# Split mixing weights kept in HBM: the high and low parts are made once and loaded in later blocks

## Chip, core and metric

One core of a Trainium2 chip runs the whole program in one launch. The metric is the device time of one execution in microseconds; lower is better.

## The reference

One decoder layer on x of 2048 positions by 1024 channels, all in float32. Its first half, the token mixer, is where the change lies:

```python
h = rms_norm(x, norm_mix_pre)
p = h @ w_in                                  # 1024 -> 2576: u, v, q, k, b_v, g, lr
out_a = gelu(u) * spatial_gate(layer_norm(gelu(v)))    # within chunks of 128 positions
o_b = gated_linear_attention(q, k, b_v, log_sigmoid(lr @ w_gk + b_gk) / 16)
out_b = rms_norm(o_b) * silu(g)
mix = concat(out_a, out_b) @ w_out            # 1024 -> 1024
x = x + rms_norm(mix)
# then: up projection, causal convolution over 3 positions, gelu gate, down projection
x = x + rms_norm(conv_ffn(rms_norm(x)))
```

## The kernel before

**Blocks.** The mixer (`mix_phase`) works on four blocks of 512 positions, b0 to b3. In each block the normalised input lies transposed in SBUF as eight tiles of 128 channels, and every weight matrix of `w_in` and `w_out` is read from HBM again. A matrix comes in pieces of about 128 x 1024 values. A block needs 28 pieces: `g0` (2), `qk` (4), `g1` (2), `g` (4), `va` (4), `u` (4), and the two halves `mx0` and `mx1` of the output projection (8), which belong to the block before and run inside this one. The output projection of b3 has no next block: its first piece is used at the end of the mixer, the other seven at the start of the FFN phase (the tail, here), from a pool of their own.

**Split.** Matmuls run in a float32 form that keeps fewer bits, so each operand is cut in a high and a low part and a product takes three matmuls: high x high, high x low, low x high. `weight()` (L82) does this for a piece: a DMA from the queue of SP (L86) brings it into a raw tile (two buffers), ACT casts it into the high part (L89), and the low part is raw minus high (L77), made by POOL for every other piece of up to 1024 columns and by DVE for the rest. High and low tiles have three buffers each in the mixer, two each in the tail.

**Names.** In the profile a piece of the weight `gw` in block b2 is `rb2gw` (raw), `hb2gw` (high) and `lb2gw` (low). `b2g0a`, `b2g1a`, `b3mx0a` and the like are accumulators. `z`, `cum`, `kd`, `qk`, `kps`, `dps`, `lv`, `os` and `ot` are steps of the linear attention: gates (L286 to L296), decays and products with them (L440 to L468), transposes and scores on PE (L495 to L532), the normalised output (L558) and its transpose (L568). `sz` (L381) is the spatial gate, fed by the normalised `va` (L368). `h0x` to `h7x` and `h0t` to `h7t` are loads and transposes of finished positions that b3 makes for the FFN; `x0m`, `x0x` and so on are the steps of the residual sum in b1 and b2. `tal` are the loads of FFN operands in the tail.

**Order.** In the mixer a scheduler of the language sets each engine's order from estimated times; the weight steps have high priority. Each engine then works strictly in its order, and so does the queue of SP: a DMA that waits for its buffer holds all that stand behind it. The attention steps (`main`) and the weight steps (`side`) are woven by ratio, so that PE has weight matmuls to do while the others prepare attention operands. The FFN phase after the tail has a written order and is not touched.

Of the kernel before, what the change touches and what calls it, by code (L numbers as in the profile page):

```python
# [7 lines left out]
F32 = mybir.dt.float32  # L8
F32R = mybir.dt.float32r
# [8 lines left out]
P = 128  # L18
D = 1024
# [18 lines left out]
def layer_kernel(ctx, tc, x, xT, w_ch, w_gl, w_tk, w_o, w_up, w_dn, w_gk, wsT, cols, conv, rows, sgub,  # L38
                 lvl, tri, sel, out):
    nc = tc.nc  # L40
# [12 lines left out]
    def scratch(shape, name):  # L53
        return dram.tile(shape, F32, tag=name, name=name)
# [21 lines left out]
    def split_lo(eng, lo, full, hi):  # L76
        eng.tensor_tensor(out=lo, in0=full, in1=hi.bitcast(F32), op=ALU.subtract)  # L77
# [1 line left out]
    wcount = [0]  # L79
    wpool = []  # L80

    def weight(src, n, name):  # L82
        pool = wpool[-1]
        with tc.high_priority():
            raw = pool.tile([P, 1056], F32, tag="wraw", name=f"r{name}", bufs=2)
            nc.sync.dma_start(out=raw[:, :n], in_=src)  # L86
            hi = pool.tile([P, 1056], F32R, tag="whi", name=f"h{name}")
            lo = pool.tile([P, 1056], F32R, tag="wlo", name=f"l{name}")
            A.copy(out=hi[:, :n], in_=raw[:, :n])  # L89
            wcount[0] += 1  # L90
            split_lo(G if wcount[0] % 2 and n <= 1024 else V, lo[:, :n], raw[:, :n], hi[:, :n])
        return hi, lo

    def rstd_of(ms, n, inv, name, tag="rstd"):
# [14 lines left out]
            PE.matmul(ps, lhsT=hi[:, sl], rhs=hl[kt], start=False, stop=False)  # L109
            PE.matmul(ps, lhsT=lo[:, sl], rhs=hh[kt], start=False, stop=(kt == KT - 1))  # L110

    def token_steps(srcs, kper, n, hh, hl, name, done):
        nk = kper * len(srcs)
        ps = [bank(f"{name}a{t}", acc=True) for t in range(TT)]
        for i, src in enumerate(srcs):
            hi, lo = weight(src, kper * n, f"{name}w{i}")
            for t in range(TT):
                for j in range(kper):
                    kt = i * kper + j
                    a = hh[kt][:, t * P:(t + 1) * P]  # L120
                    b = hl[kt][:, t * P:(t + 1) * P]
                    sl = slice(j * n, (j + 1) * n)
                    PE.matmul(ps[t][:, :n], lhsT=a, rhs=hi[:, sl], start=(kt == 0), stop=False)
                    PE.matmul(ps[t][:, :n], lhsT=a, rhs=lo[:, sl], start=False, stop=False)
                    last = PE.matmul(ps[t][:, :n], lhsT=b, rhs=hi[:, sl], start=False, stop=(kt == nk - 1))
                if i == len(srcs) - 1:
                    done(t, ps[t])
            yield last.ins
# [18 lines left out]
    def mix_phase(mp, late):  # L147
# [39 lines left out]
        for i in range(2):  # L187
            t = one.tile([P, 2, NH, P], F32, name=f"attn{i}")
# [13 lines left out]
        def gl_pieces(g, per):  # L202
            return [w_gl[g, :, i * per * 264:(i + 1) * per * 264] for i in range(KT // per)]

        def mix_in(b, prev):
            n = f"b{b}"
# [50 lines left out]
            def evac_lr(t, ps):  # L257
# [4 lines left out]

            per = 2 if b == 0 else 4
            g0 = token_steps(gl_pieces(0, per), per, 264, hh, hl, f"{n}g0",
                             lambda t, ps: held.append((t, ps)))
            held = []
            for i in range(4):
                load_pair(i)
# [30 lines left out]
            qT = w1.tile([P, 2, T], F32, tag="qT", name=f"{n}q", bufs=1)  # L299
            kT = w1.tile([P, 2, T], F32, tag="kT", name=f"{n}k", bufs=1)  # L300
            for i in range(4):
                hi, lo = weight(w_ch[i], D, f"{n}qk{i}")
                ps = bank(f"{n}qk{i}")
                chan_mm(ps, hi, lo, hh, hl)
                if i == 0:
                    rs.extend(token_scales())
                    for h in held:
                        evac_lr(*h)
                if i == 1:
                    rb = spread_scales()  # L310
                    V.scalar_tensor_tensor(out=qT[:, 0, :], in0=first, scalar=0.125, in1=rb,
                                           op0=ALU.mult, op1=ALU.mult)
                first = ps
                if i == 1:
                    V.scalar_tensor_tensor(out=qT[:, i, :], in0=ps, scalar=0.125, in1=rb,
                                           op0=ALU.mult, op1=ALU.mult)
                elif i > 1:
                    V.tensor_tensor(out=kT[:, i - 2, :], in0=ps, in1=rb, op=ALU.mult)
                if i == 1:
                    gates()  # L320
# [15 lines left out]
            def side():  # L336
                def gate(t, ps):
                    A.activation(out=sg[t], in_=ps, func=AF.Silu, scale=rs[t][:, 0:1])

                yield from token_steps(gl_pieces(1, 4), 4, 264, hh, hl, f"{n}g1", evac_v)  # L340
                yield from token_steps([w_tk[0, i] for i in range(4)], 2, 512, hh, hl, f"{n}g", gate)
                def g4(nm):
                    return w1.tile([P, D], F32, tag="xin", name=nm, bufs=4)

                if prev is not None:
                    for k, ins in enumerate(mix_out(b - 1, *prev)):
                        if b == 3 and k % 2 == 0:
                            xs = h_load(0, k // 2, g4)
                        yield
                        if b == 3 and k % 2:  # L350
                            with tc.issue_after(ins):
                                h_combos(0, k // 2, xs, g4, g4,
                                         lambda nm: [bank(f"{nm}{k}") for k in range(2)])
                            yield
                    if b < 3:
                        yield from x1_steps(b - 1, gpost, lambda nm: w1.tile([P, D], F32, tag="xin", name=nm, bufs=4))

                va = [w1.tile([P, 512], F32, tag="va", name=f"{n}va{t}", bufs=4) for t in range(TT)]

                def norm_va(t, ps):  # L360
                    v = va[t]
                    A.activation(out=v, in_=ps, func=AF.Gelu, scale=rs[t][:, 0:1])
                    st = w1.tile([P, 6], F32, tag="bns", name=f"{n}st{t}", bufs=4)
                    mv = w1.tile([P, 2], F32, tag="bna", name=f"{n}mv{t}", bufs=4)
                    V.bn_stats(out=st, in_=v)
                    V.bn_aggr(out=mv, in_=st)
                    r = rstd_of(mv[:, 1:2], 1, 1.0, f"{n}lr{t}")
                    V.tensor_scalar(out=v, in0=v, scalar1=mv[:, 0:1], scalar2=r[:, 0:1],  # L368
                                    op0=ALU.subtract, op1=ALU.mult)

                yield from token_steps([w_tk[1, i] for i in range(4)], 2, 512, hh, hl, f"{n}va", norm_va)
                for h in range(NH):
                    hi, lo = weight(w_ch[4 + h], D, f"{n}u{h}")
                    ps = bank(f"{n}u{h}")
                    chan_mm(ps, hi, lo, hh, hl)
                    u = w1.tile([P, T], F32, tag="u", name=f"{n}u{h}")
                    V.tensor_tensor(out=u, in0=ps, in1=rb, op=ALU.mult)
                    A.activation(out=u, in_=u, func=AF.Gelu)
                    zp = bank(f"{n}sz{h}")
                    for t in range(TT):  # L380
                        PE.matmul(zp[:, t * P:(t + 1) * P], lhsT=va[t][:, h * P:(h + 1) * P],  # L381
                                  rhs=ws_sb[:, h, :], start=True, stop=True)
                    z = w1.tile([P, T], F32, tag="z", name=f"{n}zs{h}", bufs=1)
                    V.scalar_tensor_tensor(out=z.rearrange("p (c t) -> p c t", c=TT),
                                           in0=zp.rearrange("p (c t) -> p c t", c=TT),
                                           scalar=c_lng[:, h:h + 1],
                                           in1=ch_sb[:, h:h + 1, :].to_broadcast([P, TT, P]),
                                           op0=ALU.mult, op1=ALU.add)
                    V.tensor_tensor(out=z, in0=z, in1=u, op=ALU.mult)
                    A.copy(out=oh[h], in_=z)  # L390
                    split_lo(V, ol[h], z, oh[h])
                    yield
# [14 lines left out]
        def mix_out(b, oh, ol):  # L407
            n = f"b{b}"
            for half in range(2):
                def evac(t, ps):  # L410
                    m = late.tile([P, 512], F32, tag="mo", name=f"{n}mo{t}", bufs=2)
                    A.copy(out=m, in_=ps)
                    A.activation(out=ps, in_=ps, func=AF.Square, accum_out=ssm[:, b, half, t:t + 1])
                    nc.scalar.dma_start(out=mix_d[b][t * P:(t + 1) * P, half * 512:(half + 1) * 512],
                                        in_=m)

                yield from token_steps([w_o[half, i] for i in range(4)], 2, 512, oh, ol,
                                       f"{n}mx{half}", evac)

        prev = None  # L420
        for b in range(NB):
# [848 lines left out]
```

## Time and profile before

| | |
|---|---|
| median of 3 runs | 2183.48 us (2183.38 to 2191.66) |
| profiled execution | 2185.53 us |
| its span, first to last instruction | 2183.7 us |
| PE busy in the span | 2091.9 us, 96% |
| DVE, ACT, POOL busy | 1559.5, 965.4, 712.1 us |
| granted TensorE clock, mean | 0.983 |
| HBM read, written | 245.26, 100.40 MB |

The mixer lies from 0 to 806 us (b1 from 168, b2 from 374, b3 from 584), the tail from 806 to 866, the FFN after it. Matmuls overlap each other and their ends are modelled, so the busy time of PE is a union of their records, and the time in which PE does nothing is the difference to the stretch.

### The profile page before, as it was taken

Reading aid. Unit: us, or ns where it says so; the run is one execution under the profiler, and the core shown is the slowest. Engines: PE = TensorE matmul, PEld = TensorE weight load, DVE = VectorE, ACT = ScalarE, POOL = GpSimd, SP = SyncE. Lnnn points to the kernel's source line nnn. Section 1 sums busy time; section 2 is a strip of 40 time slices with the busy share of each in tenths; the row PEclk is TensorE's granted clock in tenths of the full one; section 3 lists DMA queues with packets and bytes.
Section 4 is the critical chain, followed back from the end, with each engine's and each line's share of the span. In section 5 each row is a group of like instructions: output and inputs, shape, how many; then the busy total and the mean of one; then the engine's idle time right before and its main releaser. Section 6 shows DMA issues by size and latency. Waiting matters only on the chain.

```text
span 2183.7 us, 27160 instructions
## 1 busy us (share of the span) xinstructions
PE 2091.9 (96%) x9904; PEld 1729.6 (79%) x9904; DVE 1559.5 (71%) x2056; ACT 965.4 (44%) x1544; POOL 712.1 (33%) x485
## 2 busy tenths in 40 slices
PE   8999999999999899999999997999999999999998
PEld 7887887887888777788888876877787778888886
DVE  6776757656766455888778879999999943434467
ACT  5445545444545635444555553334333333322352
POOL 3322323123222123555545555555555300000000
PEclk9999999999999999999999998999999999999999
DMA  8422245225424636445445463434444543444467
GB/s 278 137 67 86 70 164 174 69 82 173 151 86 127 199 102 238 165 172 195 137 154 181 149 225 111 166 130 163 164 148 149 199 159 131 159 146 156 142 239 262
DMA packets 140518, 338.80 MB, mean 155 GB/s; under 512 B 13136, under 2 KB 42208, under 8 KB 140384
## 3 DMA queue, kind: packets, MB, share of 16 engines
q1 hardware_dynamic: 135488, 328.57, 44.6%
q10 hardware_dynamic: 4896, 8.50, 1.1%
q8 instruction: 78, 1.28, 0.2%
q14 instruction: 56, 0.46, 0.1%
HBM read 245.26 MB, written 100.40 MB: 158 GB/s over the span
## 4 chain that ended last, share of the span: by engine, by line
PE 60%; DVE 23%; issue 6%; ACT 5%; DMA 4%; POOL 2%; SPq 0%; DVEq 0%; POOLq 0%; ACTq 0%
PE d0C L1109 3%; PE d0D L1109 3%; PE d1A L1109 3%; PE d1C L1109 3%; PE d0A L1109 2%; PE d1D L1109 2%; PE d1B L1109 1%; PE d0B L1109 1%; DVE klow L468 1%; DVE ds L602 1%; DVE dw L601 1%; DVE dw L603 1%; DVE attn L484 1%; PE u01G L746 1%; PE u015G L746 1%
## 5 line engine op out<-in xcount | busy, mean ns | idle before, releaser
L1089 POOL TENSOR_TENSOR o01r<-o01r,mhalf 128x4 f32<-128x4 f32 x1 | 1.0, 1006 | 358.7 <-DVE o01r L1088 358.7
L77 DVE TENSOR_TENSOR tal<-tal,tah 128x1024 fp32r<-128x1024 f32 x14 | 25.5, 1864 | 6.6 <-ACT tah L679 6.6
L77 DVE TENSOR_TENSOR d05tl<-d05tl,d05th 128x1024 fp32r<-128x1024 f32 (+1 forms) x6 | 6.6, 1134 | 20.2 <-ACT d05th L679 20.1
L77 DVE TENSOR_TENSOR d11tl<-d11tl,d11th 128x1024 fp32r<-128x1024 f32 (+1 forms) x6 | 6.6, 1134 | 19.9 <-ACT d11th L679 19.9
L1065 DVE TENSOR_TENSOR r<-d0C,du 128x512 f32<-128x512 f32 x8 | 5.2, 686 | 21.6 <-PE d0C L1109 21.6
L1109 PE MATMUL d0A<-d0wh,d00th 128*128 128x512 f32 x44 | 17.8, 405 | 2.8 <-DVE u121y L773 2.8
L1109 PE MATMUL d0A<-d0wl,d00th 128*128 128x512 f32 x44 | 17.9, 408 | 2.6 <-DVE d0wl L77 2.6
L77 DVE TENSOR_TENSOR d01tl<-d01tl,d01th 128x1024 fp32r<-128x1024 f32 (+1 forms) x6 | 6.6, 1134 | 18.5 <-ACT d01th L679 18.5
L77 DVE TENSOR_TENSOR tbl<-tbl,tbh 128x1024 fp32r<-128x1024 f32 x10 | 13.1, 1353 | 9.0 <-ACT tbh L679 9.0
L77 DVE TENSOR_TENSOR d10tl<-d10tl,d10th 128x1024 fp32r<-128x1024 f32 (+1 forms) x6 | 6.6, 1134 | 17.4 <-ACT d10th L679 17.4
L679 ACT CAST tah<-tal 128x1024 fp32r<-128x1024 f32 x14 | 14.6, 1047 | 8.1 <-DMA tal<-act 8.1
L1109 PE MATMUL d0A<-d0wh,d00tl 128*128 128x512 f32 x44 | 17.9, 406 | 0.0
L603 DVE TENSOR_TENSOR dw<-dw,ds 128x512 f32<-128x512 f32 x11 | 17.4, 1581 | 0.4
L601 DVE TENSOR_TENSOR dw<-dw 128x512 f32<-128x512 f32 x11 | 17.4, 1579 | 0.4
L602 DVE TENSOR_TENSOR ds<-dw,dw 128x512 f32<-128x512 f32 x11 | 17.4, 1579 | 0.4
L1109 PE MATMUL d1B<-d5wh,d15th 128*128 128x512 f32 x44 | 17.1, 389 | 0.0
L1109 PE MATMUL d0C<-d3wl,d03th 128*128 128x512 f32 x44 | 17.1, 389 | 0.0
L1109 PE MATMUL d1A<-d1wh,d11tl 128*128 128x512 f32 x44 | 17.1, 389 | 0.0
L1109 PE MATMUL d1C<-d6wh,d16tl 128*128 128x512 f32 x44 | 17.1, 389 | 0.0
L1109 PE MATMUL d1D<-d4wh,d14tl 128*128 128x512 f32 x44 | 17.1, 389 | 0.0
L1109 PE MATMUL d1A<-d0wh,d10th 128*128 128x512 f32 x44 | 17.1, 389 | 0.0
L1109 PE MATMUL d0A<-d1wh,d01tl 128*128 128x512 f32 x44 | 17.1, 389 | 0.0
(4559 smaller groups left out, 8422.7 us busy)
## 6 DMA issues: line engine op xcount, KB each, us to landing
dw<-in_w_dn SPq DMA_DIRECT2D x22, 512.0 KB, 5.2
tal<-act SPq DMA_DIRECT2D x14, 512.0 KB, 7.1
tbl<-act SPq DMA_DIRECT2D x14, 512.0 KB, 6.3
wdn<-in_w_dn SPq DMA_DIRECT2D x6, 1024.0 KB, 7.8
out<-r SPq DMA_DIRECT2D x12, 512.0 KB, 7.5
wdn<-dw SPq DMA_DIRECT2D x22, 256.0 KB, 2.3
wdn<-ds SPq DMA_DIRECT2D x22, 256.0 KB, 3.0
d00tl<-ffs SPq DMA_DIRECT2D x5, 512.0 KB, 8.0
```

The costliest lines, as they stand in the source:

```text
L77: eng.tensor_tensor(out=lo, in0=full, in1=hi.bitcast(F32), op=ALU.subtract)
L468: V.tensor_tensor(out=view(kl)[:, :, :, 0, :], in0=view(k)[:, :, :, 0, :], in1=ev[:, :, :, 0, :], op=ALU.mult)
L484: V.copy_predicated(out=av[:, :, :, 1, :], mask=mk.unsqueeze(1).to_broadcast([P, 8, gc, s]), data=ps.rearrange("p (x g s) -> p x g s", x=8 ...
L601: eng.tensor_tensor(out=b12, in0=b12, in1=b11, op=ALU.subtract)
L602: eng.tensor_tensor(out=t2, in0=b22, in1=b12, op=ALU.subtract)
L603: eng.tensor_tensor(out=t4, in0=b21, in1=t2, op=ALU.subtract)
L679: A.copy(out=hi[:, sl], in_=raw[:, sl])
L746: ins = PE.matmul(ps, lhsT=a[:, sl], rhs=b[:, i], start=not more and i == 0 and k == 0, stop=i == 3 and k == 2, skip_group_check=more)
L1065: return V.tensor_tensor(out=row(half, o[0], t)[:, o[1] * T:(o[1] + 1) * T], in0=ps, in1=u, op=ALU.add)
L1089: G.tensor_tensor(out=rs, in0=rs, in1=mhalf[:, :4], op=ALU.pow)
L1109: ins = PE.matmul(ps, lhsT=lhs, rhs=wop[w][:, i], start=start and k == 0, stop=stop and k == 2, skip_group_check=more)
```

## The change

`weight()` takes a key. The first call with a key splits the piece as before and then writes both parts to HBM (two more DMAs on the queue of SP, without the high priority). Each later call with that key loads the two parts straight into the high and low tiles: no raw tile, no cast, no subtraction. All weights of the mixer have keys but `g0` in b0, which is cut in another way there; `g0`, `mx0` and `mx1` are therefore first kept in b1, the rest in b0.

```diff
-    def weight(src, n, name):
+    kept = {}
+
+    def weight(src, n, name, key=None):
         pool = wpool[-1]
         with tc.high_priority():
+            hi = pool.tile([P, 1056], F32R, tag="whi", name=f"h{name}")
+            lo = pool.tile([P, 1056], F32R, tag="wlo", name=f"l{name}")
+            if key in kept:
+                for t, d in zip((hi, lo), kept[key]):
+                    nc.sync.dma_start(out=t[:, :n].bitcast(F32), in_=d)
+                return hi, lo
             raw = pool.tile([P, 1056], F32, tag="wraw", name=f"r{name}", bufs=2)
             nc.sync.dma_start(out=raw[:, :n], in_=src)
-            hi = pool.tile([P, 1056], F32R, tag="whi", name=f"h{name}")
-            lo = pool.tile([P, 1056], F32R, tag="wlo", name=f"l{name}")
             A.copy(out=hi[:, :n], in_=raw[:, :n])
             wcount[0] += 1
             split_lo(G if wcount[0] % 2 and n <= 1024 else V, lo[:, :n], raw[:, :n], hi[:, :n])
+        if key is not None:
+            kept[key] = [scratch([P, n], f"k{name}{i}") for i in range(2)]
+            for t, d in zip((hi, lo), kept[key]):
+                nc.sync.dma_start(out=d, in_=t[:, :n].bitcast(F32))
         return hi, lo
...
-            hi, lo = weight(src, kper * n, f"{name}w{i}")
+            hi, lo = weight(src, kper * n, f"{name}w{i}", key and (key, i))
...
-                hi, lo = weight(w_ch[i], D, f"{n}qk{i}")
+                hi, lo = weight(w_ch[i], D, f"{n}qk{i}", ("qk", i))
```

The other calls get their keys in the same way. Of 114 calls, 32 still split, 28 of them also write (56 DMAs), and 82 load (164 DMAs in place of 82). ACT loses 82 casts, DVE 46 and POOL 36 subtractions. Lines behind L82 stand some ten further down in the changed kernel.

The scheduler makes another order of it. On PE in b2, at the gates, the order before was as follows (`b2g1a` accumulates `g1`, `b2z` are the gates, `b2qk` a piece of `qk`):

```order
L123 MATMUL b2g1a_3663<-hb2g1w_3668,b2hi_3264 128x264
L124 MATMUL b2g1a_3663<-lb2g1w_3669,b2hi_3264 128x264
L125 MATMUL b2g1a_3663<-hb2g1w_3668,b2lo_3265 128x264
L123 MATMUL b2g1a_3663<-hb2g1w_3668,b2hi_3271 128x264
L286 MATMUL b2z_3520<-b2lrT,wg_sb 128x512
L286 MATMUL b2z_3524<-b2lrT,wg_sb 128x512
L108 MATMUL b2qk_3545<-b2hi_3260,hb2qk_3541 128x512
L109 MATMUL b2qk_3545<-b2lo_3261,hb2qk_3541 128x512
```

and the order now, at the same place:

```order
L118 MATMUL b2qk_3541<-b2hi_3430,hb2qk_3537 128x512
L119 MATMUL b2qk_3541<-b2lo_3431,hb2qk_3537 128x512
L120 MATMUL b2qk_3541<-b2hi_3430,lb2qk_3538 128x512
L256 MATMUL b2rb<-ident,b2rep 128x128 x4
L288 MATMUL b2lrT<-ident,b2lr 16x128 x4
L296 MATMUL b2z_3588<-b2lrT,wg_sb 128x512
L296 MATMUL b2z_3592<-b2lrT,wg_sb 128x512
L118 MATMUL b2qk_3611<-b2hi_3336,hb2qk_3607 128x512
```

21 matmuls of the first `g1` piece, which stood ahead of the gates, now stand behind the `qk` pieces. On DVE in b2 the order from the gates (`b2zm`) over the running sum (`b2cum`) to the attention operands was:

```order
L292 TENSOR_TENSOR b2zm<-b2zm,b2ze 128x1024
L296 SCALAR_TENSOR_TENSOR b2cum<-ones,b2zm 128x128 x5
L77 TENSOR_TENSOR lb2g1w_3736<-rb2g1w_3733,hb2g1w_3735 128x1056
L296 SCALAR_TENSOR_TENSOR b2cum<-ones,b2zm 128x128 x3
L318 TENSOR_TENSOR b2k<-b2qk_3545,b2rb 128x512
L435 COPY b2h0last<-b2h0eb 128x4
L440 TENSOR_TENSOR b2h0kd<-b2cum 128x512
L436 TENSOR_TENSOR b2h0eb<-b2h0eb,b2q 128x512
L318 TENSOR_TENSOR b2k<-b2qk_3577,b2rb 128x512
L443 TENSOR_TENSOR b2h0kd<-b2h0kd,b2k 128x512
L445 TENSOR_TENSOR b2h0qk<-b2q,b2k 128x512
```

and now:

```order
L302 TENSOR_TENSOR b2zm<-b2zm,b2ze 128x1024
L306 SCALAR_TENSOR_TENSOR b2cum<-ones,b2zm 128x128 x8
L328 TENSOR_TENSOR b2k<-b2qk_3611,b2rb 128x512
L445 COPY b2h0last<-b2h0eb 128x4
L450 TENSOR_TENSOR b2h0kd<-b2cum 128x512
L446 TENSOR_TENSOR b2h0eb<-b2h0eb,b2q 128x512
L328 TENSOR_TENSOR b2k<-b2qk_3641,b2rb 128x512
L453 TENSOR_TENSOR b2h0kd<-b2h0kd,b2k 128x512
L455 TENSOR_TENSOR b2h0qk<-b2q,b2k 128x512
```

The subtraction for the second `g1` piece is gone from between the running sums. In the queue of SP at the start of the tail (`rb3mx0w` are raw pieces, `u0rg` and `u0rv` FFN weights, `tal` FFN operands) the order was:

```order
L86 DMA rb3mx0w_6764<-in_w_o 128x1024
L86 DMA rb3mx0w_6831<-in_w_o 128x1024
L86 DMA rb3mx0w_6869<-in_w_o 128x1024
L684 DMA u0rg<-in_w_up 128x1024
L685 DMA u0rv<-in_w_up 128x1024
L86 DMA rb3mx0w_6907<-in_w_o 128x1024
L86 DMA rb3mx1w_6965<-in_w_o 128x1024
```

and now, where `kb0mx0w` are the kept parts in HBM:

```order
L91 DMA hb3mx0w_6728<-kb0mx0w_2405 128x1024
L91 DMA lb3mx0w_6729<-kb0mx0w_2406 128x1024
L91 DMA hb3mx0w_6793<-kb0mx0w_2460 128x1024
L91 DMA hb3mx0w_6829<-kb0mx0w_2520 128x1024
L91 DMA lb3mx0w_6794<-kb0mx0w_2461 128x1024
L91 DMA lb3mx0w_6830<-kb0mx0w_2521 128x1024
L694 DMA u0rg<-in_w_up 128x1024
L695 DMA u0rv<-in_w_up 128x1024
L682 DMA tal_6786<-act_89 128x1024
L91 DMA lb3mx0w_6866<-kb0mx0w_2573 128x1024
L91 DMA hb3mx0w_6865<-kb0mx0w_2572 128x1024
```

Four loads of parts stand where two raw loads stood, both high parts first. Loads of the third piece now wait for PE to be done with the first, since there are two buffers and no raw tile ahead of them.

## Rows read from the trace of the kernel before

**Rows 1.** The page: busy time, share of the span and instructions of each engine.

```profile
PE 2091.9 (96%) x9904; PEld 1729.6 (79%) x9904; DVE 1559.5 (71%) x2056; ACT 965.4 (44%) x1544; POOL 712.1 (33%) x485
```

**Rows 2.** Stretches: us, then busy of PE, PEld, DVE, ACT, POOL; granted clock; DMA.

```profile
168.00:374.00 206.00, 196.72 (x1056) 164.52 (x1055) 138.92 (x236) 100.78 (x168) 55.19 (x38) 0.99 0.38 123
374.00:584.00 210.00, 199.62 (x1059) 167.08 (x1058) 138.34 (x234) 99.76 (x166) 55.54 (x38) 0.98 0.38 121
584.00:806.00 222.00, 209.58 (x1120) 175.89 (x1119) 133.69 (x233) 114.09 (x222) 55.11 (x37) 0.96 0.39 124
806.00:866.00 60.00, 52.77 (x213) 41.71 (x212) 33.55 (x24) 33.10 (x52) 21.41 (x10) 0.91 0.62 219
```

**Rows 3.** Waits of PE in 168 to 866 us: total us, times, longest.

```profile
PE b3mx0a L123 <- ACT hb3mx0w L89: 4.8, 1, 4.8
PE b3mx1a L124 <- POOL lb3mx1w L77: 2.4, 1, 2.4
PE b2h1ot L568 <- DVE b2h1os L558: 2.3, 2, 1.9
...
PE h1t L627 <- ACT h1x L612: 2.3, 1, 2.3
...
PE b2h0dps L499 <- DVE b2h0qk L445: 2.0, 1, 2.0
...
PE b1sz L381 <- DVE b1va L368: 1.5, 2, 1.0
...
PE b2g0a L123 <- ACT b2hi L217: 1.3, 1, 1.3
...
PE b2h0kps L495 <- DVE b2h0kd L443: 1.1, 1, 1.1
...
PE b2g1a L124 <- DVE lb2g1w L77: 0.5, 1, 0.5
```

**Rows 4.** Stretches at half clock, columns as in rows 2.

```profile
217.80:221.20 3.40, 3.40 (x18) 3.40 (x17) 3.40 (x8) 1.63 (x2) 2.29 (x2) 0.50 0.26 107
422.60:429.40 6.80, 5.59 (x25) 5.59 (x26) 4.69 (x12) 1.88 (x3) 3.19 (x3) 0.50 0.22 77
```

**Rows 5.** DVE in order of time, 412 to 432 us: start, us.

```profile
415.55 1.24 DVE L77 TENSOR_TENSOR lb2g1w<-rb2g1w,hb2g1w 128x1056 fp32r<-128x1056 f32 x1
...
420.31 0.69 DVE L443 TENSOR_TENSOR b2h0kd<-b2h0kd,b2k 128x512 f32<-128x512 f32 x1
420.92 2.84 DVE L445 TENSOR_TENSOR b2h0qk<-b2q,b2k 128x512 f32<-128x512 f32 x1
```

**Rows 6.** POOL in order of time, the same stretch.

```profile
420.74 2.47 POOL L77 TENSOR_TENSOR lb2gw<-rb2gw,hb2gw 128x1024 fp32r<-128x1024 f32 x1 [24.44 <-ACT hb2gw L89]
```

**Rows 7.** DVE in order of time, 346 to 358 us.

```profile
349.27 2.62 DVE L368 TENSOR_SCALAR b1va<-b1va,b1mv,b1lr 128x512 f32<-128x512 f32 x1 [1.09 <-POOL b1lr L97]
```

**Rows 8.** POOL in order of time, the same stretch.

```profile
349.20 2.40 POOL L77 TENSOR_TENSOR lb1u<-rb1u,hb1u 128x1024 fp32r<-128x1024 f32 x1
```

**Rows 9.** DMA issues, 0 to 870 us: count, KB each, us to landing.

```profile
tal<-act SPq DMA_DIRECT2D x14, 512.0 KB, 7.1
...
rb2qk<-in_w_ch SPq DMA_DIRECT2D x4, 512.0 KB, 3.5
...
mix<-b3mo ACTq DMA_DIRECT2D x8, 256.0 KB, 2.0
...
h5x<-x SPq DMA_DIRECT2D x1, 512.0 KB, 7.2
```

**Rows 10.** PE in order of time, 356 to 372 us.

```profile
360.36 1.05 PE L381 MATMUL b1sz<-ws_sb,b1va 128*128 128x128 f32 x8
...
366.84 1.05 PE L381 MATMUL b1sz<-ws_sb,b1va 128*128 128x128 f32 x8
```

**Rows 11.** The queue of SP in order of time, 798 to 845 us.

```profile
812.13 0.80 SPq L86 DMA_DIRECT2D rb3mx0w<-in_w_o  x2
```

**Rows 12.** A stretch, columns as in rows 2 (last: DMA share, GB/s).

```profile
820.00:830.00 10.00, 10.00 (x41) 8.05 (x40) 7.50 (x7) 6.53 (x10) 8.12 (x6) 0.90 0.91 316
```

More of the change, by code (lines that the diff above doesn't have):

```diff
@@ L110, in chan_mm, with token_steps @@
             PE.matmul(ps, lhsT=lo[:, sl], rhs=hh[kt], start=False, stop=(kt == KT - 1))
-    def token_steps(srcs, kper, n, hh, hl, name, done):
+    def token_steps(srcs, kper, n, hh, hl, name, done, key=None):
         nk = kper * len(srcs)
@@ L264, in mix_in @@
             g0 = token_steps(gl_pieces(0, per), per, 264, hh, hl, f"{n}g0",
-                             lambda t, ps: held.append((t, ps)))
+                             lambda t, ps: held.append((t, ps)), None if b == 0 else "g0")
             held = []
@@ L338, in gate @@
                     A.activation(out=sg[t], in_=ps, func=AF.Silu, scale=rs[t][:, 0:1])
-                yield from token_steps(gl_pieces(1, 4), 4, 264, hh, hl, f"{n}g1", evac_v)
-                yield from token_steps([w_tk[0, i] for i in range(4)], 2, 512, hh, hl, f"{n}g", gate)
+                yield from token_steps(gl_pieces(1, 4), 4, 264, hh, hl, f"{n}g1", evac_v, "g1")
+                yield from token_steps([w_tk[0, i] for i in range(4)], 2, 512, hh, hl, f"{n}g", gate, "g")
                 def g4(nm):
@@ L369, in norm_va @@
                                     op0=ALU.subtract, op1=ALU.mult)
-                yield from token_steps([w_tk[1, i] for i in range(4)], 2, 512, hh, hl, f"{n}va", norm_va)
+                yield from token_steps([w_tk[1, i] for i in range(4)], 2, 512, hh, hl, f"{n}va", norm_va, "va")
                 for h in range(NH):
-                    hi, lo = weight(w_ch[4 + h], D, f"{n}u{h}")
+                    hi, lo = weight(w_ch[4 + h], D, f"{n}u{h}", ("u", h))
                     ps = bank(f"{n}u{h}")
@@ L417, in mix_out @@
                 yield from token_steps([w_o[half, i] for i in range(4)], 2, 512, oh, ol,
-                                       f"{n}mx{half}", evac)
+                                       f"{n}mx{half}", evac, f"mx{half}")
         prev = None
```

## Prediction

> **What bounds the kernel now.** I read the page first: PE is busy for 96% of the span, DVE for 71%, ACT for 44%, POOL for 33% [rows 1]. No other engine is near its limit, so work taken from DVE, ACT and POOL can pay only where PE stands still or runs slow because of them. The stretches say how much that is. PE does nothing for 206 - 196.7 = 9.3 us in b1, 10.4 in b2, 12.4 in b3 and 7.2 in the tail, 39.3 together [rows 2]. Its granted clock there is 0.99, 0.98, 0.96 and 0.91; a stretch at half clock that lasts T costs T/2, so the share missing is the time lost: 2.1 + 4.2 + 8.9 + 5.4 = 20.6 us [rows 2]. Some 60 us is thus all that the mixer behind b0 and the tail can give. The FFN is not touched, and b0 still splits everything.
>
> The waits of PE say who holds it [rows 3]: in each block DVE, before `dps` (2.0), `kps` (1.1) and the second term of `g1a` (0.5); in b1 and b2 DVE before `ot` (2.3) and `sz` (1.5); in b2 and b3 ACT before `g0a` (1.3). In the tail ACT (4.8) and POOL (2.4) hold it with the weights themselves, and in b3 the loads of `h1x` do (2.3).
>
> The timelines say why. `L445` in b2 takes 2.84 us, where `L443` of the same shape takes 0.69 [rows 5]. POOL subtracts for `lb2gw` from 420.74 for 2.47 us, to 423.21 [rows 6]; `L445` began at 420.92 and ended 0.55 after that. It stood still while POOL worked. `L368` before `sz` did so too: 2.62 us from 349.27 [rows 7], under a POOL split from 349.20 for 2.40 [rows 8]. So POOL's splits, seemingly hidden, stop DVE on its way to PE.
>
> **The change part by part.** *Removed:* 82 casts, 46 DVE and 36 POOL subtractions, about 1.1, 1.24 and 2.4 us each by my reading of such rows [rows 5, 6, 8]. Their own time is hidden under PE and counts nothing; the waits count.
>
> (a) Gates to scores, b1 to b3. The path loses the split of 1.24 between the running sums and the stop of 2.84 - 0.69 = 2.15 in `L445` [rows 5]. That is 3.4 us, more than `kps` and `dps` wait (3.1) [rows 3]. The wait of `g1a` goes because those matmuls moved behind `qk`. Gates and everything behind them move ahead together, so that the number of matmuls between gates and `kps` stays. Saved: three blocks at about 3.5, 10.5 us (b1 and b3 are within 0.2 of b2). The half clock that follows each of these waits lasted 3.4 us in b1, 6.8 in b2 [rows 4], and I take 6.8 of the four stretches in b3's 0.96 [rows 2]: 17.0 / 2 = 8.5 us, between 0 (the clock falls anyway) and 8.5. I take 8.5, since each such stretch began within a few us of a wait.
>
> (b) `sz`: 1.5, 1.5 and about 0.5 us; without the stop 2.7 of the 3.5 go. `ot`: 4.6 in two blocks; DVE's path to it loses splits, but PE's transposes were also put ten matmuls earlier; between 0 and 4.6, I take 2.6. `g0a`: ACT casts the next `qk` piece ahead of the input's last part and waits for that piece; the cast is gone, but the input's load now stands behind two more 512 KB transfers; between 0 and 3, I take 2.5. Two stretches of half clock go with these, 3.4 together, of which I take 2.5.
>
> (c) Tail. The first wait stays: the parts of the second piece can only be loaded when PE has left the first, as the raw load was at 812.13 [rows 11], and high parts of two pieces come before the low ones. The 2.4 for POOL goes, and half of a 1.7 clock loss, 0.85.
>
> *Added:* 56 stores and 82 more loads, 138 DMAs of 512 KB, 72 MB, on a queue that spends 0.4 us on each [rows 11]. What they cost PE is bounded thus. One 512 KB load lands in 3.5 us [rows 9]. At 316 GB/s with the DMA engines 0.91 busy [rows 12], full rate is about 347, and a second 512 KB takes 1.5 us more: a pair lands in about 5.1, an estimate. A pair is issued when PE is done with the piece three before, so two pieces cover it; one `u` piece with its four small matmuls takes 6.48 us [rows 10], two 13.0. Even the slowest row, 7.2 in b3 [rows 9], makes 8.7 with the second part. So zero in b1 and b2. In the tail only one piece covers, about 5.7 us without the small matmuls, against 5.1: thin, and it moves 14 parts, 2 FFN weights, 12 of 14 `tal` loads and 8 stores of 256 KB [rows 9], 16.8 MB, for which 347 GB/s need 48.4 of some 54 us. So no more than the 3.25 of (c) is there. In b3 the `h` loads queue behind 1 MB instead of 0.5, 1.5 us each in two of four rounds: a cost of 3.0 (0 to 8). For waits that the new order makes elsewhere I allow 2.0 (0 to 10). The stores of b0 and b1 wait for splits for which the raw loads behind them wait too: 0. The copies of `w_dn` move later in b0; only the down projection, 900 us on, reads them: 0.
>
> *Sum:* 10.5 + 8.5 + 2.7 + 2.6 + 2.5 + 2.5 + 2.4 + 0.85 = 32.5 saved, 5.0 added: 27.5. The profiled execution took 2185.53, so 2158.0; it lies 2.05 above the median of the runs, so **2156 us**.
>
> **Rivals.**
>
> *The parts come late (slower).* Place: the 12 pieces of b3 beside the `h` loads and stores, and the 7 of the tail. If each comes 2 us late, that is 38 us and, at two stretches of half clock as in b2 [rows 4], some 6 more: 2156 + 44 = 2200. It decides where each of the 19 is 27.5 / 19 = 1.45 us late: a pair that lands after more than 5.7 + 1.45 = 7.1 us in the tail, or 13.0 + 1.45 = 14.4 in b3, eats the whole gain. For it: the tail's thin cover. Against: 8.7 by the slowest row, with 13 of cover.
>
> *Hidden anyway (no change).* PE is at 96%, and order and transfers give new waits as old ones go: the idle time of (a) and half its clock come back, 10.5 + 4.25, and b3, tail and order take 10: 2178.7 by the median. For it: PE's order is fixed by estimates, and `ot` was put earlier. Against: rows 5 to 8, which name a stop that no longer exists. The Trainium skill (Perfetto Trace Analysis, Identifying the Most-Contended Engine) says to optimise the engine of highest occupancy first; that is PE, from which this change takes nothing, and by that rule the time would stay near 2183. The waits of PE on DVE in this trace differ from it in part.
>
> *The clock does not come back.* Waits go, the half-clock stretches stay: 8.5 + 2.5 + 0.85 are lost from the sum: 2168, still faster.
>
> *More than forecast.* All idle time but the tail's first wait and about 6 of the `h` loads, 28.4, and all clock but 3.4 for each of these, 13.8: 42.2 saved, 2141.
>
> **How the numbers follow.** A measurement of this kernel tells about 0.5%, 11 us, from no change. Forecast 0.55, clock stays 0.15, more than forecast 0.05: faster 0.75. Hidden anyway 0.16: same. Late parts 0.09: slower. The range goes from 2141 to 2178, where (a) gives only its 10.5 and 5.0 are paid (2185.5 - 5.5 - 2); beyond it lie the slower case and about half of no change.
>
> **What would show it.** `L445` at about 0.7 us in b1 to b3, no wait of 1 us before `kps` and `dps`, and the clock of b1 to b3 at 0.99 or 1.00: (a). The waits of `sz`, `ot`, `g0a` at half or less: (b). No wait on a low part in the tail beyond the first, which stays at 3.5 to 5: (c). Waits of PE on DMAs of `hb` or `lb` pieces, or `h1t` and `h2t` waiting 5 us or more, would make the prediction wrong, as would b0 growing past 168 us.

## The result

The changed kernel took 2160.81 us (median of 5 runs, 2159.9 to 2162.19), the kernel before 2189.58 beside it (5 runs, 2183.38 to 2191.66): a ratio of 0.9887, 95% interval 0.987 to 0.9903, so 1.1% faster. Forecast were 2156 us, 2141 to 2178, which against the 2183.48 shown then is a ratio of 0.9874. The profiled execution took 2162.19, 23.3 less than that of before.

The stretches of the changed kernel, b1 to b3 and the tail, then all of b1 to b3 in one (columns as in rows 2):

```profile
168.00:370.60 202.60, 198.97 (x1078) 166.86 (x1076) 117.50 (x228) 84.00 (x152) 37.89 (x30) 0.99 0.62 219
370.60:568.70 198.10, 194.37 (x1058) 163.25 (x1057) 103.66 (x218) 72.11 (x138) 28.11 (x26) 1.00 0.58 203
568.70:781.00 212.30, 204.81 (x1124) 172.25 (x1122) 102.60 (x219) 87.82 (x194) 23.47 (x24) 0.98 0.60 201
781.00:866.00 85.00, 71.11 (x282) 54.60 (x281) 31.91 (x32) 33.62 (x56) 21.70 (x14) 0.94 0.72 260
...
170.80:780.90 610.10, 595.25 (x3234) 499.69 (x3233) 320.85 (x659) 241.17 (x479) 89.47 (x80) 0.99 0.60 207
```

The same stretch of the kernel before, from the first matmul of b1 to the first of b3's output projection:

```profile
167.80:806.30 638.50, 606.42 (x3236) 507.99 (x3234) 411.45 (x701) 314.82 (x554) 165.84 (x113) 0.98 0.38 123
```

PE's idle time there went from 638.5 - 606.4 = 32.1 us to 14.9, and its busy time for the same matmuls from 606.4 to 595.3: 17.2 and 11.2 us less. Of the 11.2, 10.2 is clock: TensorE was granted half its clock (0.50, as in rows 4) for 30.7 us of this stretch before and for 10.2 us now, and half of the difference is the time won. The table takes each stage from the first matmul of its first accumulator to that of the next (b0: `b0g0a` to `b1g0a`; b1 to b3: up to `b3mx0a`; tail: up to `u01G`; rest: to the end of the span), in the profiled executions:

| us | b0 | b1 to b3 | tail | rest |
|---|---|---|---|---|
| before | 161.4 | 638.5 | 81.1 | 1296.4 |
| changed | 164.3 | 610.1 | 84.3 | 1295.1 |

So b1 to b3 gave 28.3 us, b0 and the tail took 2.9 and 3.3 back, and the rest, which is the same work, came out 1.3 shorter. The waits of PE that answer to rows 3:

```profile
PE b3mx0a L133 <- DMA hb3mx0w<-kb0mx0w: 3.8, 1, 3.8
PE u00V L756 <- ACT b3mx1a L423: 2.8, 1, 2.8
PE b0g1a L134 <- DVE lb0g1w L77: 2.7, 1, 2.7
...
PE u00V L756 <- DVE u00u L995: 2.2, 1, 2.2
PE u00G L756 <- DVE tal L77: 2.0, 2, 1.5
...
PE b3mx1a L133 <- DMA hb3mx1w<-kb0mx1w: 1.8, 2, 1.0
...
PE b1h1o L542 <- DVE attn L494: 1.4, 1, 1.4
...
PE b1sz L391 <- DVE b1va L378: 1.0, 1, 1.0
PE b3mx0a L134 <- DMA lb3mx0w<-kb0mx0w: 0.9, 1, 0.9
...
PE b2z L296 <- DVE b2lrT L290: 0.9, 1, 0.9
PE b2sz L391 <- DVE b2va L378: 0.7, 1, 0.7
...
PE b2h1ot L578 <- DVE b2h1os L568: 0.5, 1, 0.5
```

`kps`, `dps` and the second `g1a` term no longer wait in b1 to b3; `ot` and `sz` wait less; new are `z`, which has no `g1` matmuls ahead of it, the output products (`b1h1o`), and in the tail the loads of parts and, behind them, the first matmuls of the FFN (`u00V`, `u00G`). The product before `dps`, in order of time on DVE:

```profile
412.00 0.69 DVE L455 TENSOR_TENSOR b2h0qk<-b2q,b2k 128x512 f32<-128x512 f32 x1
```

It took 2.84 in rows 5.

### The profile page after: what moved, and what is told of

Read it like the earlier page. It is cut to its first block, busy times and chain, and to the rows that moved or that the text cites. A ratio compares the mean times of both kernels' runs of the same rounds, so it can differ in the third digit from the quotient of the medians.

```text
span 2160.4 us, 27160 instructions
## 1 busy us (share of the span) xinstructions
PE 2081.2 (96%) x9904; PEld 1718.5 (80%) x9904; DVE 1456.4 (67%) x2010; ACT 885.4 (41%) x1462; POOL 628.3 (29%) x449
## 4 chain that ended last, share of the span: by engine, by line
PE 42%; DVE 14%; issue 3%; DMA 1%; ACT 1%; DVEq 0%; SPq 0%; POOLq 0%; POOL 0%; ACTq 0%
PE d0D L1119 3%; PE d1C L1119 3%; PE d0C L1119 3%; PE d1A L1119 3%; PE d1D L1119 2%; PE d0A L1119 2%; PE d1B L1119 1%; PE d0B L1119 1%; DMA dw<-in_w_dn 1%; DVE dw L611 1%; DVE ds L612 1%; DVE dw L613 1%; PE u017G L756 1%; PE u015G L756 1%; PE u013G L756 1%
## 5 line engine op out<-in xcount | busy, mean ns | idle before, releaser
L77 DVE TENSOR_TENSOR tal<-tal,tah 128x1024 fp32r<-128x1024 f32 x14 | 19.8, 1422 | 25.4 <-ACT tah L689 25.4
L494 DVE COPY_PREDICATED attn<-lvl_sb,b3h1lv 128x512 f32<-128x512 uint8 x7 | 6.3, 895 | 26.2 <-PE b3h1lv L491 26.2
L474 POOL TENSOR_TENSOR qup<-b1q,b1h0e 64x256 f32<-64x256 f32 x7 | 9.8, 1406 | 41.9 <-issue 25.1
L689 ACT CAST tah<-tal 128x1024 fp32r<-128x1024 f32 x14 | 14.5, 1047 | 17.2 <-DMA tal<-act 17.2
L474 POOL TENSOR_TENSOR qup<-b2q,b2h0e 64x256 f32<-64x256 f32 x7 | 9.8, 1407 | 40.1 <-issue 23.3
L474 POOL TENSOR_TENSOR qup<-b3q,b3h0e 64x256 f32<-64x256 f32 x7 | 8.1, 1156 | 42.0 <-issue 23.4
L474 POOL TENSOR_TENSOR qup<-b2q,b2h1e 64x256 f32<-64x256 f32 x7 | 5.6, 804 | 44.7 <-PE b2h1lv L491 26.9
L474 POOL TENSOR_TENSOR qup<-b3q,b3h1e 64x256 f32<-64x256 f32 x7 | 5.7, 817 | 40.7 <-PE b3h1lv L491 35.3
L1119 PE MATMUL d1A<-d0wl,d10th 128*128 128x512 f32 x44 | 17.1, 389 | 0.0
```

The lines of the kernel that those rows point to most:

```text
L474: (G if par else V).tensor_tensor(out=qu[r, :, par, :].rearrange("p a (g s) -> p a g s", s=s), in0=view(q)[r, :, :, 1, :], in1=ev[r, :, :, ...
L494: V.copy_predicated(out=av[:, :, :, 1, :], mask=mk.unsqueeze(1).to_broadcast([P, 8, gc, s]), data=ps.rearrange("p (x g s) -> p x g s", x=8 ...
L689: A.copy(out=hi[:, sl], in_=raw[:, sl])
L1119: ins = PE.matmul(ps, lhsT=lhs, rhs=wop[w][:, i], start=start and k == 0, stop=stop and k == 2, skip_group_check=more)
```

## The experiments

My theory after the result: the time came from DVE no longer being stopped by POOL's subtractions. Its rivals: PE's new order, the work taken from DVE's own path, and the transfers themselves. The stages of all runs, measured like those above, with ratio and interval against the kernel before on the same chip:

| | b0 | b1 to b3 | tail | median | ratio |
|---|---|---|---|---|---|
| e1 keep_pool | 162.6 | 611.1 | 82.6 | 2159.05 | 0.9887 (0.9871 to 0.9904) |
| e2 keep_dve | 159.6 | 631.5 | 88.7 | 2179.42 | 0.9988 (0.997 to 1.0005) |
| e3 load_only | 160.4 | 611.2 | 87.6 | 2161.86 | 0.9901 (0.9886 to 0.9916) |
| e4 store_only | 163.6 | 639.4 | 81.7 | 2189.61 | 1.0027 (1.0015 to 1.0039) |
| e5 split_dve | 156.0 | 613.8 | 78.2 | 2155.78 | 0.9868 (0.9853 to 0.9883) |
| e6 tail_raw | 163.5 | 610.3 | 81.0 | 2159.56 | 0.9886 (0.9869 to 0.9902) |
| e7 tail3 | 163.2 | 612.8 | 82.4 | 2160.66 | 0.9895 (0.9877 to 0.9913) |
| e8 store_hp | 160.5 | 608.1 | 84.5 | 2160.7 | 0.9893 (0.9878 to 0.9908) |
| e9 pool_dummy | 165.5 | 625.4 | 83.3 | 2175.64 | 0.9957 (0.994 to 0.9974) |
| e10 split_pool | 163.7 | 655.3 | 83.5 | 2208.6 | 1.011 (1.0089 to 1.013) |
| e11 keep_best | 161.8 | 608.7 | 79.8 | 2153.33 | 0.9855 (0.9832 to 0.9877) |
| e12 split_dve | 155.7 | 613.9 | 78.6 | 2152.72 | 0.9861 (0.9834 to 0.9888) |

The runs e1 to e4, e5 to e8 and e9 to e12 shared a chip each. Where a stage did not change its program (b1 to b3 in the changed kernel, e6 and e7) it came out between 610.1 and 612.8 us, so less than 3 us in a stage of one profile tells little by itself.

**e1 and e2: which subtractions?** Each keeps one half of the pieces, by the engine that split them before.

```diff
+        wcount[0] += 1
+        on_pool = wcount[0] % 2 and n <= 1024
+        if not on_pool:          # e2: if on_pool:
+            key = None
...
-            wcount[0] += 1
-            split_lo(G if wcount[0] % 2 and n <= 1024 else V, lo[:, :n], raw[:, :n], hi[:, :n])
+            split_lo(G if on_pool else V, lo[:, :n], raw[:, :n], hi[:, :n])
```

> Only the pieces that POOL split are kept in HBM; DVE still splits the others, raw, in every block, and after b0 and b1 POOL splits nothing. PE's order at the gates is that of the kernel before (21 g1 matmuls ahead of z). Theory (the gain comes from DVE no longer being stopped by POOL's splits): the product before dps takes 0.7 us in b1 to b3 instead of 2.84, the wait before dps falls from 2.0 to under 0.5 in each block, that before kps stays near 1.0 (DVE's split between the running sums is still there), sz waits at half of 1.5; most of the 23 us come, about 2168 to 2172. Rival (the gain comes from PE's new order, with the gates put ahead of the g1 matmuls): with the old order the waits of kps and dps stay at 3 us a block and the time at 2180 or above.

> The reverse: only the pieces that DVE split are kept; POOL still splits the others in every block. PE's order at the gates is that of the changed kernel (no g1 matmul ahead of z). Theory (stops by POOL): operations of DVE that meet a POOL split still take some 2.6 to 2.9 us, waits of 1 us and more stay before dps, sz or ot, and the time is near 2175 to 2180. Rival (order): z stands 4.5 us of matmuls earlier, that covers the stop, kps and dps wait for nothing, and the time is near 2166 to 2170.

Keeping POOL's half gave the whole gain, more than the 2168 to 2172 expected; keeping DVE's half none in the whole time that can be told from zero. Of e1, b1 to b3 in one, two waits of PE, at an output product and at the gates, and DVE before `dps`:

```profile
169.10:780.30 611.20, 594.17 (x3236) 498.52 (x3234) 368.29 (x701) 282.94 (x521) 85.90 (x80) 0.99 0.49 163
```

```profile
PE b1h1o L545 <- DVE attn L497: 1.5, 1, 1.5
...
PE b2h0kps L508 <- DVE b2h0kd L456: 1.1, 1, 1.1
```

```profile
414.46 0.69 DVE L458 TENSOR_TENSOR b2h0qk<-b2q,b2k 128x512 f32<-128x512 f32 x1
```

DVE did the same 701 instructions as before in this stretch, and was busy for 368.3 us instead of 411.5: 43 us of what the profile of before calls busy were standing still. PE's order at the gates was the old one, so the order is not the cause; `kps` waits 1.1 as before, because DVE's split between the running sums is still there, and `dps` no longer waits. Of e2, the same views:

```profile
166.00:797.50 631.50, 605.72 (x3236) 509.04 (x3234) 357.46 (x659) 273.41 (x512) 162.45 (x113) 0.98 0.50 166
```

```profile
PE b2sz L394 <- DVE b2va L381: 2.2, 2, 1.9
...
PE b2h0dps L512 <- DVE b2h0qk L458: 2.0, 1, 2.0
```

```profile
L458 DVE TENSOR_TENSOR b2h0qk<-b2q,b2k x1: 2834/2834/2834, 416.0 to 416.0; 128x512 f32<-128x512 f32 x1
```

With the new order, and with 42 instructions fewer on DVE, the product again takes 2.83 us and `dps` waits 2.0: z's earlier place does not cover the stop. DVE's half is not worth nothing, though: by its profile e2 is 7.0 us shorter than before in b1 to b3, where `kps` no longer waits and `ot` hardly does, and loses 7.6 in the tail, where PE waits 6.3 us for a low part from POOL.

**e5 and e12: no transfer at all.** The kernel before with one edit:

```diff
-            split_lo(G if wcount[0] % 2 and n <= 1024 else V, lo[:, :n], raw[:, :n], hi[:, :n])
+            split_lo(V, lo[:, :n], raw[:, :n], hi[:, :n])
```

> The kernel before, nothing kept and nothing stored, with one edit: all subtractions are made by DVE and none by POOL. Theory (it is the meeting of POOL's subtractions with DVE's work that costs the time, not the subtractions as such): the product before dps takes 0.7 us in b1 to b3, the wait before dps is under 0.5, and although DVE makes 14 subtractions of 1.2 us more in each block, about as much as keep_pool saved comes, 2158 to 2166. Rival (the time comes from taking work away from DVE's path): with more on that path waits before kps, lv, ot and sz grow, 2180 or more.

> The kernel before with all subtractions on DVE, once more, on the same chip as keep_best, in more rounds: 2152 to 2157, at a ratio of 0.985 to 0.988 to the kernel before. If keeping has a worth of its own, keep_best lies 5 us or more below it.

As the theory has it, and faster than I expected of it: 0.9868 and 0.9861, with nothing kept and not one byte more through HBM. DVE of e5 in order of time, and b1 to b3 in one:

```profile
408.17 0.69 DVE L443 TENSOR_TENSOR b2h0kd<-b2h0kd,b2k 128x512 f32<-128x512 f32 x1
408.77 1.22 DVE L77 TENSOR_TENSOR lb2gw<-rb2gw,hb2gw 128x1024 fp32r<-128x1024 f32 x1
409.91 0.69 DVE L445 TENSOR_TENSOR b2h0qk<-b2q,b2k 128x512 f32<-128x512 f32 x1
```

```profile
162.50:776.30 613.80, 594.45 (x3236) 497.24 (x3234) 404.58 (x738) 314.16 (x554) 91.43 (x76) 1.00 0.40 128
```

The subtraction that POOL made beside `L445` now stands ahead of it on DVE. It costs DVE 1.2 us there; on POOL it cost DVE 2.15. With 37 instructions more than before, DVE is busy 6.9 us less.

**e9 and e10: more of it.** e9 gives the changed kernel POOL work that nobody reads; e10 gives POOL all subtractions of up to 1024 columns in the kernel before.

```diff
+    junk = const.tile([P, 256], F32R, name="junkw")
...
                     nc.sync.dma_start(out=t[:, :n].bitcast(F32), in_=d)
+                if on_pool:
+                    for c in range(0, n, 256):
+                        split_lo(G, junk, hi[:, c:c + 256].bitcast(F32), hi[:, c:c + 256])
                 return hi, lo
```

> The changed kernel, and for each of the 36 loaded pieces that POOL split before, four subtractions of 256 columns on POOL whose result nobody reads. The order on PE, DVE, ACT and in the queue of SP is row for row that of the changed kernel; nothing waits for the added work but the reuse of a high tile. Theory (DVE stands still while POOL's subtractions run): products and other DVE operations of 0.7 us in b1 to b3 take 2 us and more where they meet one, waits of 1 to 2 us come back before kps, dps, sz or ot, and 10 to 20 us of the gain are lost again: 2170 to 2180. Rival (only the subtractions' place in the chain of a weight counted): nothing waits for the result, so 2161 within 2 us.

> The kernel before with every subtraction of up to 1024 columns on POOL: about 100 instead of 50 in all, and DVE has that many less. Theory (each meeting stops DVE): twice the meetings cost up to twice as much, the time rises by 10 to 25 us to 2195 to 2210. Rival (DVE is too busy on the path): DVE has some 15 subtractions of 1.2 us less in each block, and the time falls below 2180.

e10 is 1.1% slower, though DVE has 36 instructions fewer in b1 to b3 than before and is busy longer:

```profile
170.20:825.50 655.30, 611.03 (x3235) 510.44 (x3233) 415.65 (x665) 314.22 (x554) 259.90 (x149) 0.97 0.38 120
```

e9 lost 15 of the 28 us in b1 to b3, in the range expected, but only in part for the reason expected. 10 of the 15 are idle time of PE, 5 its longer busy time. DVE's 659 instructions were busy 11.5 us longer than the changed kernel's:

```profile
172.40:797.80 625.40, 600.47 (x3236) 503.83 (x3234) 332.32 (x659) 240.77 (x479) 179.89 (x212) 0.98 0.59 202
```

`kps` and `dps` did not wait, as their product met no POOL work; the waits grew at `sz` (to 1.7 in b1 and in b2) and before the output products `b1h1o` and `b2h1o` (from 1.4 and 1.2 to 2.6 and 3.7). At the last one POOL, then DVE, in order of time:

```profile
524.57 0.61 POOL L77 TENSOR_TENSOR junkw<-hb2vaw 128x256 fp32r<-128x256 f32 x1 [4.39 <-DMA hb2vaw<-kb0vaw]
525.14 1.01 POOL L596 TENSOR_TENSOR x1rm<-x1rm,mhalf 128x4 f32<-128x4 f32 x1
526.12 2.86 POOL L77 TENSOR_TENSOR junkw<-hb2vaw 128x256 fp32r<-128x256 f32 x3
```

```profile
526.18 1.63 DVE L604 SCALAR_TENSOR_TENSOR x4m<-x4m,x1rm,gpost 128x1024 f32<-128x1024 f32 x1 [3.28 <-POOL x1rm L596]
527.74 1.28 DVE L499 COPY_PREDICATED attn<-lvl_sb,b2h1lv 128x512 f32<-128x512 uint8 x1
```

DVE waited 3.28 us for a step of four columns on POOL, which stood in POOL's order behind an added subtraction that waited 4.39 for a load. That is a second way in which work on POOL reaches PE, and e9 does not say how the 15 us divide between the two. In the kernel before the second way does not show: in b1 to b3 DVE's waits on POOL sum to 18.6 us there and to 21.5 in the changed kernel. What the kernel before had more of is the stop, the 43 us of e1.

**e3, e4 and e8: what b0 lost.** e3 leaves out all stores but those of two pieces (a `qk` and a `g1` piece, not three as its expectation has it), so that the later loads bring wrong weights; e4 adds the stores to the kernel before and loads nothing; e8 sets the stores inside the block of high priority.

```diff
             split_lo(G if wcount[0] % 2 and n <= 1024 else V, lo[:, :n], raw[:, :n], hi[:, :n])
-        if key is not None:
-            kept[key] = [scratch([P, n], f"k{name}{i}") for i in range(2)]
-            for t, d in zip((hi, lo), kept[key]):
-                nc.sync.dma_start(out=d, in_=t[:, :n].bitcast(F32))
+            if key is not None:
+                kept[key] = [scratch([P, n], f"k{name}{i}") for i in range(2)]
+                for t, d in zip((hi, lo), kept[key]):
+                    nc.sync.dma_start(out=d, in_=t[:, :n].bitcast(F32))
```

> The changed kernel with only 3 pieces written to HBM, one of each size (g0 and g1 share one); all later calls load that piece, so that most products are made with other weights than they should; traffic and order of the loads are those of the changed kernel. Theory (b0 lost 3.0 us because high and low tiles are held by stores that stand behind raw loads in the queue of SP and land late): b1 begins at about 167.8 again, the wait before the first g1 piece's low part falls from 2.7 to 0.5, and the time is about 2158. Rival (b0 lost it to PE's new order, z ahead of g1): b1 still begins at 170.8, the time stays near 2161. What b1 to b3 save is the same under both.

> The kernel before, with the stores of b0 and b1 added and no load of kept parts: every call splits, 56 DMAs of 512 KB more. Theory (stores hold the tiles): b0 ends 2 to 4 us later than 167.8 with PE's old order, and the wait before the first g1 piece's low part is 2 us or more; from b2 on everything as before, so 2187 to 2190 on a chip where before takes 2185. Rival (order): b0 ends at 168, the time is that of before within 1 us.

> The changed kernel with the stores at the weights' high priority, so that each stands in the queue of SP right behind its split. Theory (b0 lost 3.0 us because stores stood late in the queue and held the low tiles): the wait before the first g1 piece's low part falls from 2.7 to under 1, b1 begins between 168 and 169, the time is about 2158 to 2159. Rival (an early store that waits for its split holds the raw loads behind it, since the queue works in order): waits on raw pieces take its place, b1 begins at 171 or later.

In the changed kernel, the queue of SP in b0, and what the low part of the first `g1` piece waited for:

```profile
31.16 3.00 SPq L94 DMA_DIRECT2D rb0g1w<-in_w_gl  x2
34.22 0.42 SPq L101 DMA_DIRECT2D kb0qk<-lb0qk  x1
```

```profile
its engine sat idle before it (us, times) until:
  DMA kb0qk<-lb0qk: 3.5, 1
```

A store of a low part stands behind two raw loads, is issued at 34.22, and until it has landed the tile is not free for the next split: DVE stands 3.5 us, PE 2.7. The first matmul of b1 comes at 167.05 us with the stores of two pieces (e3), 167.08 with early ones (e8), 170.13 in e4 and 170.80 in the changed kernel, so the loss came with the late stores. That PE's order has no part in it is not shown. The stores change the order in b0 too, which the expectations of e3 and e4 did not foresee: PE works there in e3 in the order of the kernel before, in e4 in that of the changed kernel (21 and 4 matmuls of `g1` ahead of the gates), and in e8 in a third one, whose first product with a low part of `g1` comes at 52.0 us instead of 42.2. The wait of 3.5 us shows that the tile was held; whether another order would have covered it is open. Early stores have a price as well: PE waits 1.4 us in e8, and 2.0 in e11 below, for the load `lnb`, which is issued later there (at 56.8 and 60.9 us, in the changed kernel at 43.1). Neither e3 nor e8 brought the whole time down as expected. In e3 the tail took 87.6 instead of 84.3; its loads all read the same piece, and why they came later is open. In e8 the three stages are 5.7 us shorter together, but the median of four runs, 2160.7, doesn't show it.

**e6 and e7: what the tail lost.**

```diff
-            if key in kept:                                     # e6
+            if key in kept and not name.startswith("b3mx"):
...
-    wpool[:] = [late.enter_context(tc.tile_pool(name="wl", bufs=2, side="right"))]   # e7
+    wpool[:] = [late.enter_context(tc.tile_pool(name="wl", bufs=3, side="right"))]
```

> The changed kernel, but the 8 pieces of b3's output projection are loaded raw and split as before; all else is kept. Theory (the tail lost because a pair of loads has one piece of cover there): no wait of mx1 on a DMA, the tail from the first b3mx0 matmul to the second FFN group takes 81 to 82 us as before instead of 84.3, the time falls 2 to 3 us against the changed kernel, to about 2158. Rival (the tail is held by the loads of FFN operands and POOL's stops, whatever form its weights have): 84 us and 2161.

> The changed kernel with three buffers instead of two for each part in the tail's pool (no more memory than the kernel before used there, which had two raw tiles). Theory (one piece of cover is too little): the waits of mx1 on DMAs, 1.8 us in two, and the second wait of mx0, 0.9, go; the first wait of 3.8 stays, because it comes from memory that the mixer's pool still holds; 2158 to 2159. Rival (the DMA engines are full there, 0.93 to 0.99 from 805 to 835 us, so an earlier issue lands no earlier): waits move, 2161.

The raw tail takes 81.0 us, as long as before, and so gets the 3.3 back; three buffers get 1.9, less than one profile can tell. No load of `mx1` holds PE any more in e7, but the second wait of `mx0`, which should have gone, grew from 0.9 to 2.6. By the medians neither can be told from the changed kernel. The tail of the changed kernel, three stretches, and the loads' time from issue to landing:

```profile
805.00:815.00 10.00, 9.71 (x42) 7.31 (x40) 3.03 (x2) 5.25 (x12) 5.79 (x4) 1.00 0.99 332
815.00:825.00 10.00, 9.10 (x38) 6.99 (x38) 3.68 (x3) 4.32 (x7) 0.00 (x0) 1.00 0.96 351
825.00:835.00 10.00, 8.98 (x39) 7.21 (x39) 2.45 (x2) 3.60 (x6) 0.00 (x0) 1.00 0.93 321
```

```profile
tal<-act SPq DMA_DIRECT2D x14, 512.0 KB, 7.6
hb3mx1w<-kb0mx1w SPq DMA_DIRECT2D x4, 512.0 KB, 5.5
lb3mx1w<-kb0mx1w SPq DMA_DIRECT2D x4, 512.0 KB, 5.1
```

The DMA engines are 0.93 to 0.99 busy, and a part takes 5.1 to 5.5 us where, by the estimate of the prediction, 5.7 cover it, not counting its place in the queue.

**e11: is keeping worth anything once POOL is silent?** The changed kernel with three edits: the subtraction always on `V` as in e5, the stores as in e8, the tail as in e6.

> The changed kernel with what the runs so far point to: the remaining subtractions all on DVE, the stores at the weights' priority, the tail's 8 pieces raw and split. Theory (keeping the parts has no worth of its own, the gain is POOL's silence): the same as split_dve on this chip within 4 us, 2150 to 2157. Rival (fewer casts and subtractions on ACT and DVE are worth something more): 2148 or less, 5 us or more under split_dve.

The same as e12 within 1 us. Inside, they differ: b1 to b3 take 608.7 us with kept parts and 613.9 without, b0 161.8 and 155.7, the tail 79.8 and 78.6. So, by one profile each, keeping has a worth of about 5 us in the three blocks, and its stores cost b0 about 6. Of these 6, 5.1 are clock: b0 of e11 has 10.2 us at half clock, b0 of e12 none.

## Why the prediction was right, and where not

**(a) Gates to scores: right in mechanism and size.** The waits of `dps`, `kps` and `g1a`, 10.4 us in the three blocks, went; forecast were 10.5. The stop of `L445` was named as the cause, and e1, e2 and e5 show it, each from another side. The Trainium skill (SBUF — State Buffer, Who interferes with whom) says that DVE and GpSimd share a port pair held as an exclusive lock, and that a DVE instruction with two SBUF inputs contends with a GpSimd instruction that reads SBUF; this trace agrees, 2.84 us against 0.69, with POOL's subtraction begun 0.18 us earlier [rows 5, 6]. One part of the step was not as argued: I let DVE's split between the running sums (1.24) count as much as the stop. In e1 it stays, `kps` waits its 1.1, and the stretch is as short within 1 us; in the changed kernel `z` waits 0.9 in each block in its place.

**Clock: right.** 8.5 + 2.5 were forecast for b1 to b3; the stretches at half clock gave 10.2 there. The 0.98 in b3 is short of the 0.99 that the prediction named as a sign.

**(b): right in sum.** Of `sz` 1.8 us went (forecast 2.7), of `ot` 4.1 (2.6); `g0a` went from waits of 1.3 in b2 and b3 to one of 0.4.

**What was added, b1 to b3: right in sum, wrong in its parts.** Forecast were 3.0 for the `h` loads and 2.0 for new waits. `h1t`, `h2t` and `h3t` wait 1.8, 1.3 and 2.2 in place of 2.3, 2.1 and 1.7 (`h7t`) before: nothing. The new waits were dearer: 2.7 before `z`, 2.6 before the output products where 0.6 stood, 0.6 before one `lv`, some 5 us. Those of the output products do not come from the move of the `g1` matmuls, as e1 and e5, where these stand ahead of the gates as before, wait 1.5 and 1.6 there. Idle time fell by 17.2, forecast 13.3 net (10.5 + 2.7 + 2.6 + 2.5 - 5.0); most of the rest is 1.5 more of `ot` and 2.2 that PE waited before `lv` in b1 and b2, a wait that the sum left out.

**b0: wrong.** "The stores of b0 and b1 wait for splits for which the raw loads behind them wait too: 0" looked at the queue, and not at the tile. A store holds its tile until it has landed, and the tile is what the next split waits for: PE's wait before `g1` rose from 0.5 to 2.7 us, and b0 by 2.9.

**(c) Tail: wrong in sign.** "So no more than the 3.25 of (c) is there": POOL's 2.4 did go, but the loads of parts hold PE there for 3.8, 0.9 and 1.8 us, nearly as long as the 4.8 and 2.4 before. The rest of the loss lies behind them: the first matmuls of the FFN wait 2.8, 2.2 and 2.0 us for the end of `mx1` and for FFN operands, where before they waited once:

```profile
PE u00V L746 <- DVE u00u L985: 3.9, 1, 3.9
```

With the tail's pieces raw again (e6) the 3.3 come back. The text had the cover as thin, 5.1 against 5.7, and took the gain all the same.

The two misses, 2.9 + 6.5 = 9.4, are larger than what b1 to b3 gave beyond the forecast, 28.3 - 24.3 = 4.0 (the terms of (a) and (b), 29.3, less 5.0 added), and the rest gave 1.3, less 0.1 at the start: 27.5 - 9.4 + 4.0 + 1.3 - 0.1 = 23.3, as measured. That the errors cancel in part is luck. Two of the signs that the prediction set for being wrong did appear: b0 ended past 168 us, at 170.8, and PE waited for DMAs of `hb` and `lb` pieces.

**The rivals.** That the parts come late happened in the tail alone. Hidden anyway fell with `dps`. The clock came back. The 2178.7 of Hidden anyway does not follow from its terms (27.5 less 10.5, 4.25 and 10 leaves 2.75 saved, 2180.7 by the median), and 3.5 + 1.5 for a pair is 5.0, not 5.1; no conclusion rests on either. What no rival said is the main finding: taking POOL's subtractions away gives at least as much as the change did (0.9868 and 0.9861 against 0.9887), and writing and reading 72 MB more was not needed for it. The prediction had the stop in its first paragraphs, and priced the change by it, but did not ask what the smallest edit is that removes it.

## What to carry to other kernels

Look in the trace for one operation with two durations, and for what another engine did in the longer one: such a stop counts as busy time, so no list of that engine's waits shows it, and a subtraction that seems free on POOL can cost DVE more than making it itself (2.15 against 1.22 us here). Before adding transfers to take such work away, measure what it costs on the engine that it stops. A store that follows a split lengthens the life of its tile by its wait in the queue and its landing, so it should stand right behind the split; what stands behind it in the queue then comes later. A buffer more was not tried in the mixer.

## What the runs showed of the hardware beyond that

The stop goes both ways. In the changed kernel POOL's product of 64x256 takes 0.77 us at 414.16, and two in a row, beside DVE products that keep their 0.41, take 5.07; a DVE product of 0.42 takes 0.96 where it meets the first. POOL, then DVE, in order of time:

```profile
414.16 0.77 POOL L474 TENSOR_TENSOR qup<-b2q,b2h0e 64x256 f32<-64x256 f32 x1 [23.31 <-issue]
...
418.55 5.07 POOL L474 TENSOR_TENSOR qup<-b2q,b2h0e 64x256 f32<-64x256 f32 x2 [1.08 <-ACT b2h0e L470]
```

```profile
412.94 0.42 DVE L469 TENSOR_TENSOR b2h0e<-b2cum 128x256 f32<-128x256 f32 x1
...
414.25 0.96 DVE L469 TENSOR_TENSOR b2h0e<-b2cum 128x256 f32<-128x256 f32 x1
...
418.98 0.41 DVE L478 TENSOR_TENSOR klow<-b2k,b2h0e 128x256 f32<-128x256 f32 x1
```

The FFN of the kernel before has the same signs; a DVE product of 128x512 takes 2.83 us at 1312.30, where 0.69 is usual, with POOL at work beside it. POOL in order of time, then the product's group:

```profile
1311.79 5.53 POOL L77 TENSOR_TENSOR tbl<-tbl,tbh 128x1024 fp32r<-128x1024 f32 x2
```

```profile
L699 DVE TENSOR_TENSOR u10s<-u1rg,u1rv 128x512 f32<-128x512 f32 x1 | 2.8, 2826 | 0.0
```

Whether taking POOL's subtractions out of the FFN pays was not tried. DVE is busy, stops included, for 419 of the 440 us from 1320 to 1760, so the 0.7 us that a subtraction of 128x512 takes on DVE, or 1.2 for 128x1024, would not be free.
